# A hybrid encoder layer on one core: first-stage steps at other places, weight remainders on VectorE, output weights in other space

## The chip, the cores and the metric

The kernel is one launch on one core of a Trainium2 chip. The metric is the device time of that core in microseconds (us); lower is better. The engines are PE (TensorE, matmuls; PEld is its weight load), DVE (VectorE), ACT (ScalarE), POOL (GpSimd) and SP (SyncE, which here issues most of the DMA transfers).

## What is computed

Two request groups go through the same layer: a prompt of 2048 rows (16 tiles of 128) and a sample of 8 streams with 16 rows each (one more tile, number 16). All arithmetic is float32. Cut to what matters here:

```python
h   = rmsnorm(x, norm_mix_pre)
P   = h @ w_in                      # q, k, v, z, b, a, B, C, H
q, k, v = silu(causal_dwconv(qkv, width 4)); q, k = l2norm(q), l2norm(k)
beta, g = sigmoid(b), -exp(a_log) * softplus(a + dt_bias)
o, S    = gated_delta_rule(q, k, v, g, beta, S0)   # per chunk: (I + A)^-1, decays, state
o       = rmsnorm_head(o) * silu(z)
y       = B * causal_dwconv(C * H, width 3)
x = x + rmsnorm_post(concat(o, y) @ w_o)
x = x + rmsnorm_post2(swiglu(rmsnorm_pre2(x)))
```

## The kernel before

To keep float32 accuracy, every large matmul is done three times on rounded parts: a tile is split into a rounded copy ("hi", made by ACT) and its remainder ("lo", a subtraction), and hi x hi, hi x lo and lo x hi are summed.

**Three stages.** The first stage (to about 971 us in the profile) makes the input projection and the gated delta rule. The second, `o_tile` (its matmuls are L1008), multiplies by `w_o`. Then come the feed-forward matmuls (L1224, L1382), which the change does not touch.

**The first stage.** The 17 tiles go in five groups: 0 to 2; 3 to 6; 7 to 10; 11, 12 and the sample tile 16; 13 to 15. For each group the 28 column blocks of `w_in` follow each other in the order four k, four q, four z, four v, then four times C, H, B. A block is 24 matmuls (L300), eight k slices with three products each, issued in three parts of 9, 9 and 6. A part with what follows it is a *step*, so that a group has 84 steps, numbered from 0; block n has the steps 3n to 3n+2. Behind a block's last part, `finish_block` takes its result out of PSUM (convolution: R, then acc by three taps at L304, then SiLU into kT, qT or vraw by ACT at L338), and `fetch` asks for the weights three blocks on. The transposes of a k, q or v block (L345) come behind the first part of the block two places later.

**The steps between the blocks.** `plan` writes down at which step each piece of the delta rule is issued. Its function `after(us)` turns a time into a number of steps by an assumed length of a step (2.3 us in group 0, 2.5 or 1.95 in the others). TensorE executes exactly this order (`manual_schedule`); the other engines get an order from the build's scheduler that follows the program's order where the operands allow it. Each engine works through its own queue in order, so that an instruction whose operand is late holds up everything behind it. The pieces are, with their lines:

- `gate_products` (L152 by its helper, scaled at L439 and L440 into xk) and `gate_rates` (three transposes at L447, then small operations); `gate_sums`; `gate_decay`, which sends a row to memory and reads it back as dt;
- `decay_mask` (L516, then an exponential at L518), `decay_scale` (L522), `key_norms`, and per tile `pair_keys`: four products k k^T (L538), taken out into AU by DVE (L539). There are two gbank buffers, so the third pair waits for the first AU;
- `solve_load` (four copies by ACT at L560, a transpose at L562) and `solve`: 31 dependent pairs of small DVE instructions (L571, L573); `solve_store` transposes the result into utd (L578); `level_a` to `level_d` then build the inverse on TensorE (L593, L610, L632, L643);
- `chunk`: per tile four parts that advance the state S; the second to last ends in `out_norm` (L654), the last, `out_turn`, transposes the output (L659) through the single obank, which L684 of the next chunk also uses;
- `sample_start` and `sample_head` in group 3: per head a load of eight states (st, two buffers, L728), two copies by POOL, 16 + 16 matmuls (L736), two further parts, and the stores of the new states;
- `x_rows_load` to `x_split`: rows and columns of the next group.

**Weights.** `weights` fills one of three w2 buffers. In group 0 (for every fourth block in group 1) it reads `w_in` in two halves into one of four wr buffers, ACT rounds each (L277), and L280 subtracts: the first eight second halves on DVE, everything else on POOL. The result is also stored, and later groups only load it (L269).

**The output projection.** Behind the first stage's last block the tiles of `op` and `oa` take the space of the first stage's hi, lo, weight and work tiles; a tile may be written once the tiles under it are done with. Within a pool, tiles lie in the order in which they are first asked for. Weight slices k=0 and k=1 (`early_w`) and the first tile's input (`early_m`) have been loaded before, in `ahead`, into free parts of U, AU, dt, kt, vt and sz. woh0 then lies on hi tiles, which the last block still reads; the staging tiles `wor` lie on work tiles of the convolutions.

`rstd` (L144, L146) is the helper for the inverse root mean square; its two small tiles have a tag from the caller.

Of the kernel before, what the change touches and what calls it, by code (L numbers as in the profile page):

```python
# [9 lines left out]
F32 = mybir.dt.float32  # L10
F32R = mybir.dt.float32r
# [6 lines left out]
P = 128  # L18
D = 1024
# [62 lines left out]
def kernel(  # L82
# [59 lines left out]
    def rstd(small, ss, n, scale, eps, tag):  # L142
        m = small.tile([P, n], F32, tag=tag + "m", name=tag + "m")
        V.tensor_scalar(out=m, in0=ss, scalar1=scale, scalar2=eps, op0=ALU.mult, op1=ALU.add)  # L144
        r = small.tile([P, n], F32, tag=tag + "r", name=tag + "r")
        G.tensor_tensor(out=r, in0=m, in1=neghalf[:, :n], op=ALU.pow)  # L146
        return r
# [9 lines left out]
    with ExitStack() as ph:  # L157
# [101 lines left out]

        wlo = [0]  # L260
        wloads = []
        stores = []

        def weights(j, gi):
            w2 = wp.tile([P, 2, KD, P], F32R, tag="w2", name="w2", bufs=3)
            wh, wl = w2[:, 0], w2[:, 1]
            late = j % 4 == 3
            if not (gi <= late or (gi == RAWG and j % 2)):
                wloads.append(nc.sync.dma_start(out=w2.bitcast(F32), in_=wsplit[j]))  # L269
                while stores:  # L270
                    stores.pop()()
                return wh, wl
            for q in range(2):
                c = slice(4 * q, 4 * q + 4)
                wr = wp.tile([P, KD // 2, P], F32, tag="wr", name="wr", bufs=4)
                wload = nc.sync.dma_start(out=wr, in_=w_in[j, :, c])
                A.copy(wh[:, c], wr)  # L277
                e = V if q and wlo[0] < 8 else G
                wlo[0] += q
                e.tensor_tensor(out=wl[:, c], in0=wr, in1=wh[:, c].bitcast(F32), op=ALU.subtract)  # L280
            wloads.append(wload)
            while stores:
                stores.pop()()
            if gi == late:
                stores.append(lambda: nc.sync.dma_start(out=wsplit[j], in_=w2.bitcast(F32)))
            return wh, wl
# [437 lines left out]
        def sample_head(g, i, h):  # L724
            c = slice(i * P, (i + 1) * P)
            kz, qz, kl, r, yt, o = (smp[nm] for nm in ("kz", "qz", "kl", "r", "yt", "o"))
            st = wk.tile([P, NS, P], F32, tag="st", name="st", bufs=2)
            tc.keep_in_program_order(nc.sync.dma_start(out=st, in_=state[:, h].rearrange("s k v -> k s v")))  # L728
            G.tensor_copy(kz[:, :, 0:LS], sl(g["kT"][h][:, c]))
            G.tensor_copy(qz[:, :, 0:LS], sl(g["qT"][h][:, c]))  # L730
# [38 lines left out]
        def plan(g, nx, events):  # L769
# [3 lines left out]
            def at(t, f, *a):  # L773
                events.setdefault(t, []).append(lambda: f(*a))
# [7 lines left out]
            if gi:  # L782
                at(2, gate_products, g)
            at(5, gate_rates, g)
            t = 5 + after(11)
            at(t, gate_sums, g)
# [4 lines left out]
            at(17, key_norms, g)  # L791
            t += after(6)
            for i in range(n):
# [6 lines left out]
            for b in range(4):  # L800
                at(t + after(5 * b), solve, g, range(8 * b, min(31, 8 * b + 8)))
            t += after(22 if gi else 28)
            at(t, solve_store, g)
            t += after(4)
            for f in (level_a, level_b, level_c, level_d):
# [4 lines left out]
            if npr < n:  # L810
                at(t, sample_start, g, npr)
                for h in range(H):
                    u = t + 1 + 5 * h
                    thread((u, u + 3, u + 5, u + 7, u + 9), sample_head(g, npr, h))
                at(u + 10, lambda: out_norm(g, npr, smp["o"]))
                at(u + 14, lambda: out_turn(g, npr, smp["o"]))
            for i in range(npr):
                thread((t, t + hop, t + 2 * hop, t + 4 * hop), chunk(g, i))
                t += 3 * hop
# [146 lines left out]
        gpost = op.tile([P, D], F32, name="gpost")  # L966
        nc.sync.dma_start(out=gpost, in_=rows_[0].partition_broadcast(P))
        ojunk = op.tile([P, 512], BF16, name="ojunk")
        woh, wol = [], []
        for k in range(KD):  # L970
            wh = oa.tile([P, D], F32R, name=f"woh{k}")
            wl = oa.tile([P, D], F32R, name=f"wol{k}")
            if k < len(early_w):
# [4 lines left out]
            else:  # L978
# [3 lines left out]
                V.tensor_sub(wl, wr, wh.bitcast(F32))  # L982
            woh.append(wh)
            wol.append(wl)

        def o_tile(t):
            if t == 0:
                mr = early_m
            else:
                m = oa.tile([P, KD, P], F32, tag="mr", name="mr")  # L990
                mr = m[:, 0:4], m[:, 4:8]
                nc.sync.dma_start(out=mr[0], in_=mixo[t])
                gi, i = PLACE[t]
                nc.sync.dma_start(out=mr[1], in_=mixs[gi][:, :, i * P:(i + 1) * P])
# [28 lines left out]
            r = rstd(op, ss[:, 2:3], 1, 1.0 / D, EPS, "oy")  # L1023
            hx = op.tile([P, D], F32, tag="hx", name="hx")
            V.tensor_scalar_mul(hx, xt, r)
            ht = op.tile([P, KD, P], F32, tag="ht", name="ht")
            for n in range(2):
# [514 lines left out]
```

## Time and profile before

| what | us |
|---|---|
| median of 3 runs | 2588.16 |
| lowest and highest | 2586.38, 2588.73 |
| the profiled execution's own time | 2589.22 |
| its span, first to last instruction | 2587.4 |
| PE busy | 2487.6 (96%) |
| DVE busy | 1669.2 (65%) |
| ACT busy | 978.7 (38%) |
| POOL busy | 687.0 (27%) |

A line of the profile names the source line, the engine and the tiles written and read: "PE gbank L538 <- DVE AU L539" is a matmul at L538 into gbank that could not start before the DVE instruction at L539 on AU had ended. A table of stretches gives, for each stretch of the span, how long each engine was busy in it, with the number of instructions, and then the mean clock granted to TensorE (1.00 is full), the busy share of the DMA engines and GB/s. Busy times include matmuls at a lowered clock, so that a busy TensorE is not always one at full speed.

### The profile page before, as it was taken

The page shows a single profiled execution, that of the slowest core. Times are in us where ns is not written, and L with a number is a line of the kernel's source. Part 1 is how long each engine was busy: PE and PEld are TensorE (multiplying, and loading weights), DVE is VectorE, ACT ScalarE, POOL GpSimd, SP SyncE. Part 2 cuts the span into 40 slices and gives each one's busy share as a digit, 9 for nine tenths or more (in the row PEclk, how much of TensorE's full clock was granted, in tenths as well). Part 3 has the DMA queues.
Part 4 walks back from the last instruction along what each step waited for, and adds up shares of the span by engine and source line. Part 5 has one row for each costly group of instructions (what it writes and reads, how often), then busy time and mean ns, then how long its engine had stood idle before and what let it go on. Part 6 is the DMA issues. An engine that isn't in the chain of part 4 may idle for free.

```text
span 2587.4 us, 39334 instructions
## 1 busy us (share of the span) xinstructions
PE 2487.6 (96%) x14366; PEld 2271.3 (88%) x14366; DVE 1669.2 (65%) x3044; ACT 978.7 (38%) x2095; POOL 687.0 (27%) x741
## 2 busy tenths in 40 slices
PE   7799999999899999999999999999999999999998
PEld 6788788888888997889999999999999988788786
DVE  6866655755754745777887764544655564777588
ACT  5435424424423414444434442222433245333343
POOL 3353121110110100215556500000000035455563
PEclk9899999999999999999999999999999999999999
DMA  6576365456656556579877788878988853343465
GB/s 231 195 238 248 146 214 193 160 184 216 226 202 206 208 173 208 194 239 319 296 257 269 262 285 257 270 241 254 295 281 284 281 157 116 106 123 124 128 219 185
DMA packets 287393, 561.91 MB, mean 217 GB/s; under 512 B 26652, under 2 KB 175328, under 8 KB 269920
## 3 DMA queue, kind: packets, MB, share of 16 engines
q1 hardware_dynamic: 165808, 483.06, 55.6%
q10 hardware_dynamic: 121392, 76.34, 9.5%
q8 instruction: 113, 1.85, 0.3%
q14 instruction: 80, 0.66, 0.1%
HBM read 400.62 MB, written 158.70 MB: 216 GB/s over the span
## 4 chain that ended last, share of the span: by engine, by line
PE 77%; DVE 12%; DMA 4%; ACT 3%; issue 2%; POOL 1%; ACTq 0%; SPq 0%; DVEq 0%; POOLq 0%
PE fbank L1224 33%; PE dbank L300 20%; PE fbank L1382 11%; PE tbank L1008 3%; PE dbank L1008 3%; DVE Ts L573 1%; DVE pr L571 1%; DVE acc L304 1%; DVE acc L1341 1%; PE gbank L736 1%; PE tbank L345 1%; DMA dr<-in_w_dn 1%; DMA partd<-pt 1%; DVE xr L1401 1%; PE gbank L688 1%
## 5 line engine op out<-in xcount | busy, mean ns | idle before, releaser
L1224 PE MATMUL fbank<-xh,fw 128*128 128x384 f32 (+1 forms) x3696 | 901.2, 327 | 7.7 <-ACT m L1258 3.8
L300 PE MATMUL dbank<-hi,w 128*128 128x384 f32 (+1 forms) x2240 | 681.3, 372 | 9.1 <-ACT w L277 7.6
L1224 PEld LDWEIGHTS fbank<-xh,fw 128*128 128x128 f32 x3696 | 653.6, 189 | 9.1 <-ACT m L1258 4.6
L1224 PE MATMUL fbank<-xl,fw 128*128 128x384 f32 (+1 forms) x1848 | 603.8, 327 | 0.0
L1382 PE MATMUL fbank<-dw,as 128*128 128x512 f32 x1980 | 461.0, 394 | 8.0 <-ACT dw L1079 2.5
L300 PEld LDWEIGHTS dbank<-hi,w 128*128 128x128 f32 x2240 | 423.8, 193 | 47.6 <-ACT w L277 7.6
L1382 PEld LDWEIGHTS fbank<-dw,as 128*128 128x128 f32 x1980 | 371.6, 188 | 97.0 <-ACT dw L1079 3.7
L300 PE MATMUL dbank<-lo,w 128*128 128x384 f32 (+1 forms) x1120 | 407.7, 364 | 1.5 <-DVE lo L213 1.5
L1224 PEld LDWEIGHTS fbank<-xl,fw 128*128 128x128 f32 x1848 | 348.5, 189 | 0.0
L1366 POOL TENSOR_TENSOR as<-ar,as 128x256 fp32r<-128x256 f32 (+1 forms) x207 | 186.5, 911 | 282.4 <-ACT as L1363 281.7
L300 PEld LDWEIGHTS dbank<-lo,w 128*128 128x128 f32 x1120 | 216.0, 193 | 21.2 <-DVE lo L213 4.1
L1341 DVE TENSOR_TENSOR acc<-acc,fbank 128x512 f32<-128x512 f32 x248 | 166.1, 681 | 95.9 <-PE fbank L1382 78.1
L1081 POOL TENSOR_TENSOR dw<-dr,dw 128x512 fp32r<-128x512 f32 x52 | 76.7, 1487 | 484.1 <-ACT dw L1079 483.8
L1363 ACT CAST as<-ar 128x256 fp32r<-128x256 f32 (+1 forms) x288 | 118.2, 427 | 187.2 <-PE fbank L1382 133.6
L304 DVE SCALAR_TENSOR_TENSOR acc<-R,cw,acc 128x384 f32<-128x384 f32 (+2 forms) x180 | 129.0, 719 | 64.9 <-ACT acc L334 58.6
L1199 ACT CAST fw<-rg 128x512 fp32r<-128x512 f32 x124 | 77.3, 623 | 194.1 <-PE fbank L1224 158.3
L1271 DVE TENSOR_TENSOR c<-u,fbank 128x384 f32<-128x384 f32 (+1 forms) x66 | 34.8, 528 | 106.1 <-PE fbank L1224 106.0
L280 POOL TENSOR_TENSOR w<-wr,w 128x512 fp32r<-128x512 f32 x62 | 86.7, 1413 | 60.0 <-ACT w L277 49.9
L1267 DVE TENSOR_TENSOR m<-m,m 128x384 f32<-128x384 f32 (+1 forms) x44 | 23.1, 525 | 93.9 <-ACT m L1260 93.8
L1269 ACT ACTIVATE m<-fbank 128x384 f32<-128x384 f32 (+1 forms) x66 | 31.3, 474 | 129.1 <-PE fbank L1224 126.0
L1200 POOL TENSOR_TENSOR fw<-rg,fw 128x512 fp32r<-128x512 f32 x44 | 70.0, 1591 | 32.7 <-ACT fw L1199 28.7
L1200 DVE TENSOR_TENSOR fw<-rg,fw 128x512 fp32r<-128x512 f32 x80 | 56.4, 706 | 15.6 <-ACT fw L1199 13.2
(360 smaller groups left out, 3488.5 us busy)
## 6 DMA issues: line engine op xcount, KB each, us to landing
w<-wsplit SPq DMA_DIRECT2D x105, 1024.0 KB, 4.9
fw<-fsplit SPq DMA_DIRECT2D x188, 512.0 KB, 4.7
fsplit<-fw SPq DMA_DIRECT2D x94, 512.0 KB, 4.3
partd<-pt ACTq DMA_DIRECT2D x88, 384.0 KB, 6.9
rg<-in_w_gu SPq DMA_DIRECT2D x62, 512.0 KB, 4.1
wsplit<-w SPq DMA_DIRECT2D x28, 1024.0 KB, 4.9
ar<-partd SPq DMA_DIRECT2D x48, 384.0 KB, 3.3
wr<-in_w_in SPq DMA_DIRECT2D x70, 256.0 KB, 4.6
```

The lines of the kernel that those rows point to most:

```text
L280: e.tensor_tensor(out=wl[:, c], in0=wr, in1=wh[:, c].bitcast(F32), op=ALU.subtract)
L300: T.matmul(ps[:, :c], l[:, k, :], r[k][:, :c], start=(k == 0 and r is hi and l is wh), stop=(k == KD - 1 and l is wl))
L304: r = V.scalar_tensor_tensor(acc, raw(d), w[:, d:d + 1], acc, op0=ALU.mult, op1=ALU.add)
L1008: T.matmul(pss[n], m_[:, j, :], w_[k][:, n * 512:(n + 1) * 512], start=(k == 0 and ci == 0), stop=(k == KD - 1 and ci == 2))
L1081: e.tensor_tensor(out=w[:, 1], in0=v, in1=w[:, 0].bitcast(F32), op=ALU.subtract)
L1199: A.copy(w[:, 0], v)
L1200: e.tensor_tensor(out=w[:, 1], in0=v, in1=w[:, 0].bitcast(F32), op=ALU.subtract)
L1224: T.matmul(ps, w_[:, c], b_[k][:, :hw], start=(first and k == 0 and ci == 0), stop=(k == KH - 1 and ci == 2), skip_group_check=not first)
L1341: V.tensor_add(dst, dst, ps)
L1363: ins = A.copy(a[:, 0, :n], v)
L1366: e.tensor_tensor(out=a[:, 1, :n], in0=v, in1=a[:, 0, :n].bitcast(F32), op=ALU.subtract)
L1382: T.matmul(ps, a[:, x_, q * P:(q + 1) * P], w[:, y_], start=(start and q == 0 and ci == 0), stop=(q == c - 1 and ci == 2), skip_group_chec ...
```

## The change

It has four parts.

1. In `weights`, all 70 subtractions go to VectorE; 62 of them were on POOL.
2. In `plan`, steps move. In group 0 `gate_rates` goes from step 5 to 8, and the first pair from 21 to 26, the solve's store from 40 to 45, `level_a` from 42 to 48, the first chunk from 52 to 57. In groups 1 and 2 the first pair goes from 20 to 22, the store from 35 to 39, `level_a` from 37 to 42; the chunks stay at 52. In groups 3 and 4 the store goes from 45 to 47, `level_a` from 48 to 51, the chunks from 57 to 60. A chunk's last part comes two steps later within its chunk. The sample's heads follow each other after seven steps in place of five, and each head's state load is issued two steps ahead of its copies.
3. Ahead of the output projection, the tiles are asked for in another order: hx, ht and mr first, then the weight slices from k=7 down to k=0. So woh0 and wol0 come to lie on the four wr buffers, the other slices from k=1 on the three w2 buffers and then on hi and lo tiles, mh on xk tiles, and the staging `wor` on vraw and xt tiles. The load of gpost moves behind the weight loads.
4. In `rstd`, the first small tile takes only the first letter of the caller's tag, so that two callers in the output projection share one, and the pool is 32 bytes smaller.

```diff
-        m = small.tile([P, n], F32, tag=tag + "m", name=tag + "m")
+        m = small.tile([P, n], F32, tag=tag[0] + "m", name=tag + "m")
...
-                e = V if q and wlo[0] < 8 else G
-                wlo[0] += q
-                e.tensor_tensor(out=wl[:, c], in0=wr, in1=wh[:, c].bitcast(F32), op=ALU.subtract)
+                V.tensor_tensor(out=wl[:, c], in0=wr, in1=wh[:, c].bitcast(F32), op=ALU.subtract)
...
             tc.keep_in_program_order(nc.sync.dma_start(out=st, in_=state[:, h].rearrange("s k v -> k s v")))
+            yield
             G.tensor_copy(kz[:, :, 0:LS], sl(g["kT"][h][:, c]))
...
-            at(5, gate_rates, g)
-            t = 5 + after(11)
+            t = 5 if gi else 8
+            at(t, gate_rates, g)
+            t += after(11)
             at(t, gate_sums, g)
...
             at(17, key_norms, g)
-            t += after(6)
+            t += after(6) + (2 if n == MAXT or not gi else 0)
...
-            t += after(22 if gi else 28)
+            t += after(26 if gi else 28)
             at(t, solve_store, g)
-            t += after(4)
+            t += after(6)
...
-                    u = t + 1 + 5 * h
-                    thread((u, u + 3, u + 5, u + 7, u + 9), sample_head(g, npr, h))
+                    u = t + 1 + 7 * h
+                    thread((u - (2 if h else 0), u, u + 3, u + 5, u + 7, u + 9), sample_head(g, npr, h))
                 at(u + 10, lambda: out_norm(g, npr, smp["o"]))
-                at(u + 14, lambda: out_turn(g, npr, smp["o"]))
+                at(u + 15, lambda: out_turn(g, npr, smp["o"]))
             for i in range(npr):
-                thread((t, t + hop, t + 2 * hop, t + 4 * hop), chunk(g, i))
+                thread((t, t + hop, t + 2 * hop, t + 4 * hop + 2), chunk(g, i))
...
-        nc.sync.dma_start(out=gpost, in_=rows_[0].partition_broadcast(P))
         ojunk = op.tile([P, 512], BF16, name="ojunk")
-        woh, wol = [], []
+        spare = [op.tile([P, D], F32, tag="hx", name="hx"), op.tile([P, KD, P], F32, tag="ht", name="ht"),
+                 oa.tile([P, KD, P], F32, tag="mr", name="mr")]
+        wo = {k: [oa.tile([P, D], F32R, name=f"{nm}{k}") for nm in ("woh", "wol")] for k in reversed(range(KD))}
+        woh, wol = ([wo[k][q] for k in range(KD)] for q in range(2))
         for k in range(KD):
-            wh = oa.tile([P, D], F32R, name=f"woh{k}")
-            wl = oa.tile([P, D], F32R, name=f"wol{k}")
+            wh, wl = wo[k]
...
+        nc.sync.dma_start(out=gpost, in_=rows_[0].partition_broadcast(P))
```

The first `o_tile` that uses hx, ht and mr takes the three tiles of `spare`.

More of the change, by code (lines that the diff above doesn't have):

```diff
@@ L258, in x_split @@
             split(nx["xk"][k], k, len(tiles) * P, nx["hi"], nx["lo"])
-        wlo = [0]
         wloads = []
@@ L982 @@
                 V.tensor_sub(wl, wr, wh.bitcast(F32))
-            woh.append(wh)
-            wol.append(wl)
+        nc.sync.dma_start(out=gpost, in_=rows_[0].partition_broadcast(P))
         def o_tile(t):
@@ L989, in o_tile @@
             else:
-                m = oa.tile([P, KD, P], F32, tag="mr", name="mr")
+                m = oa.tile([P, KD, P], F32, tag="mr", name="mr") if t > 1 else spare[2]
                 mr = m[:, 0:4], m[:, 4:8]
@@ L1023, in o_tile @@
             r = rstd(op, ss[:, 2:3], 1, 1.0 / D, EPS, "oy")
-            hx = op.tile([P, D], F32, tag="hx", name="hx")
+            hx = op.tile([P, D], F32, tag="hx", name="hx") if t else spare[0]
             V.tensor_scalar_mul(hx, xt, r)
-            ht = op.tile([P, KD, P], F32, tag="ht", name="ht")
+            ht = op.tile([P, KD, P], F32, tag="ht", name="ht") if t else spare[1]
             for n in range(2):
```

## The prediction

> **What bounds the kernel now.** I read the page first, then the waits of TensorE between 21 and 981 us (the first stage without its start), then a table of stretches, then single lines.
>
> ```profile
> span 2587.4 us, 39334 instructions
> ```
>
> ```profile
> PE gbank L538 <- DVE AU L539: 11.5, 3, 6.3
> PE gbank L593 <- DVE utd L578: 11.0, 3, 5.2
> PE gbank L736 <- DMA st<-in_state: 8.3, 2, 4.8
> PE tbank L345 <- DVE R L311: 5.3, 1, 5.3
> PE tbank L345 <- ACT qT L338: 4.9, 4, 3.2
> PE gbank L447 <- ACT xk L440: 3.8, 1, 3.8
> PE dbank L1008 <- ACT mh L1002: 3.7, 1, 3.7
> PE tbank L345 <- ACT kT L338: 2.8, 3, 2.2
> PE obank L659 <- DVE o L684: 2.5, 2, 2.1
> PE obank L659 <- DVE o L654: 2.3, 1, 2.3
> ```
>
> These ten rows say that TensorE sat idle some 56 us, in about a dozen places, and who ended each wait (columns: total us, times, longest). The change moves the steps behind most of them. Next the stretches: first the groups 0, 1, 3 and 4, then a window around each wait. Columns: length, busy PE, PEld, DVE, ACT, POOL, then the granted clock.
>
> ```profile
> 0.00:217.00 217.00, 180.63 (x1156) 167.92 (x1157) 154.24 (x297) 97.53 (x190) 90.41 (x101) 0.93 0.67 233
> 217.00:424.00 207.00, 201.97 (x1246) 168.57 (x1245) 127.81 (x259) 82.80 (x156) 41.44 (x57) 0.98 0.54 192
> ```
> ```profile
> 624.00:818.00 194.00, 176.60 (x1164) 167.81 (x1162) 114.33 (x302) 64.56 (x158) 22.09 (x52) 0.95 0.60 205
> 818.00:971.00 153.00, 149.18 (x1086) 144.48 (x1084) 85.74 (x213) 55.27 (x116) 16.56 (x37) 0.99 0.57 199
> 33.00:42.00 9.00, 6.18 (x23) 6.05 (x24) 5.60 (x18) 7.04 (x11) 0.61 (x2) 0.62 0.41 161
> 60.00:126.00 66.00, 49.81 (x316) 47.64 (x315) 57.55 (x118) 28.17 (x48) 29.90 (x31) 0.88 0.55 188
> 71.00:90.00 19.00, 9.41 (x35) 8.58 (x35) 14.00 (x22) 9.78 (x13) 5.39 (x7) 0.73 0.40 149
> 116.00:131.00 15.00, 8.64 (x164) 7.57 (x162) 11.04 (x23) 8.07 (x16) 6.51 (x11) 0.66 0.53 176
> 165.00:172.00 7.00, 4.85 (x20) 3.55 (x19) 3.75 (x5) 0.99 (x3) 3.06 (x2) 0.76 0.82 267
> 263.00:271.00 8.00, 5.42 (x25) 4.38 (x24) 4.46 (x8) 1.93 (x4) 0.27 (x2) 0.79 0.00 0
> 300.00:308.00 8.00, 5.56 (x80) 4.60 (x80) 4.05 (x12) 4.76 (x8) 0.51 (x1) 0.79 0.01 2
> 470.00:477.00 7.00, 4.42 (x28) 3.63 (x27) 4.76 (x8) 2.19 (x4) 0.37 (x2) 1.00 0.08 12
> 703.00:715.00 12.00, 6.77 (x102) 6.19 (x102) 5.96 (x17) 6.37 (x16) 0.49 (x2) 0.72 0.41 145
> 770.00:780.00 10.00, 6.51 (x35) 6.38 (x35) 4.30 (x10) 0.63 (x1) 0.83 (x3) 0.66 0.78 270
> 790.00:800.00 10.00, 5.25 (x27) 5.29 (x28) 0.04 (x1) 0.00 (x0) 0.00 (x0) 0.66 0.34 118
> 896.00:906.00 10.00, 6.70 (x164) 5.92 (x162) 4.44 (x11) 5.00 (x10) 0.64 (x2) 0.83 0.27 103
> 971.00:981.00 10.00, 6.32 (x16) 4.97 (x17) 6.25 (x9) 5.83 (x9) 0.00 (x0) 0.66 0.71 229
> ```
>
> A wait costs more than its idle time: in eleven of these twelve windows the granted clock fell too. I price a window as length minus PE busy, plus PE busy times (1 minus clock). 71:90 gives 9.6 + 9.41 x 0.27 = 12.1 us. In order of time: 33:42 5.2; 71:90 12.1; 116:131 9.3; 165:172 3.3; 263:271 3.7; 300:308 3.6; 470:477 2.6; 703:715 7.1; 770:780 5.7; 790:800 6.5; 896:906 4.4; 971:981 5.8. Together **69.3 us**; with the 2.3 us for L654, 71.6 us. No more than that is to be had here.
>
> By the Trainium skill, TensorE: Matmul & The Clock Gate, section "HAM oscillation", only idle gaps over about 3.4 us throttle the clock. Idle of 2.15, 2.58 and 2.44 us (165:172, 263:271, 300:308) came with clocks of 0.76 to 0.79 here, and 2.58 us at 470:477 with 1.00, so the measurement decides and short gaps can count. By the rule those three windows and 896:906 (3.30 us idle) would lose 4.6 us less, and the forecast below would be about 2549.
>
> **The change, part by part.** A step is a third of a block; a group has 84. From PE busy over 84, one lasts about 2.15 us in group 0, 2.4 in 1 (and 2), 2.1 in 3, 1.8 in 4.
>
> *Remainders to VectorE.* 62 subtractions leave POOL:
>
> ```profile
> L280 POOL TENSOR_TENSOR w<-wr,w x62: 1257/1298/1748, 7.6 to 402.1; 128x512 fp32r<-128x512 f32 x62
> ```
> ```profile
> L280 DVE TENSOR_TENSOR w<-wr,w x8: 676/1362/1732, 8.1 to 55.9; 128x512 fp32r<-128x512 f32 x8
> ```
>
> Undisturbed, VectorE takes 0.68 us: 62 x 0.68 = 42.2 us more for it, 48 of the 62 in group 0. Against that stands what POOL does to VectorE. The same 31 + 31 solve instructions (L571, then L573), in group 0 with 12 POOL remainders beside them and in group 4 with none:
>
> ```profile
> 87.00:123.50 36.50, 12.38 (x31) 0.92 0.53 173
> 871.00:900.00 29.00, 7.86 (x31) 1.00 0.60 218
> ```
> ```profile
> 87.00:123.50 36.50, 12.96 (x31) 0.92 0.53 173
> 871.00:900.00 29.00, 8.62 (x31) 1.00 0.60 218
> ```
> ```profile
> 87.00:123.50 36.50, 14.33 (x12) 0.92 0.53 173
> ```
>
> 25.3 against 16.5 us: 8.9 us lost to 12 remainders, 0.74 each; the 12 would cost VectorE 8.2. So I take the move as **zero** for VectorE's load, with ends of +42.2 us (no relief) and -3.7 us (62 x 0.06). A block's weights are fetched two blocks ahead, about 10 us in group 0; that covers a remainder queued behind the solve unless VectorE lags further than that.
>
> By the Trainium skill, TensorE: Matmul & The Clock Gate, section "Architectural detail", VectorE's queue is strictly first in, first out, so a remainder cannot pass the taps and solve steps ahead of it. No row here shows such a lag reaching a block's weights; if it did by some 5 us once, the forecast would be about 2550.
>
> *Group 0's gate step, 5 to 8 (window worth 5.2).* The transposes at L447 no longer wait for the gates' scaling.
>
> ```profile
> 35.82 0.50 PE L447 MATMUL gbank<-cst,xk 16*128 16x16 f32 x3 [3.76 <-ACT xk L440]
> ```
> ```profile
> 37.08 0.52 ACT L338 ACTIVATE kT<-acc 128x384 f32<-128x384 f32 x1
> ```
>
> TensorE is free at 35.82 - 3.76 = 32.06 and now runs block 2's first nine matmuls, until about 34. What is late next is the transposition of the first k block, which needs kT, done at 37.6. So the wait mostly changes its name. Gain **2** (0 to 5.2).
>
> *Group 0's pairs, solve and levels, five or six steps later (windows 71:90 and 116:131, worth 21.4).* For the third pair, five steps are 10 us against 6.3 of idle, and the decay mask behind it comes only three steps later. But 60:126 shows VectorE busy 57.55 of 66 us, so this stretch can shrink by little more than the 8.5 us in which VectorE idles. And the solve's store, from step 40 to 45, now stands behind the taps of two more v blocks. TensorE will still wait before the levels, only with more blocks behind it. Gain **8** (-5 to 18).
>
> *A chunk's last part two steps later.* The output transposes no longer stand in front of L684 and L654: two steps are 4 us against 2.1 and 2.3 us of idle. Gain **3** in group 0 (of 3.3) and **1.5** in group 3 (of 2.3), ends zero and the whole.
>
> *Groups 1 and 2.* Pairs two steps later (4.8 us, idle 2.6 each); levels five steps later (12 us, idle 2.4); the chunks stay at step 52, so there is slack behind. Group 1's 14 remainders net to zero as above. Gains **7** of 7.3 (4 to 7.3) and **2.5** of 2.6 (1 to 2.6).
>
> *Groups 3 and 4: levels three steps later.* 6.3 and 5.4 us against 5.23 and 3.30 us of idle, so the move alone covers them. But the solve's store goes from step 45 to 47, behind the last v block's three taps of about 0.6 us each: the wait returns by up to 2 us, with its clock. Gains **4** of 7.1 (1 to 7.1) and **3** of 4.4 (1 to 4.4).
>
> *Sample heads every seven steps instead of five, each state load two steps ahead of its copies (windows 770:780 and 790:800, worth 12.2).*
>
> ```profile
> DMA to landing us min/median/max: 6.7/6.8/7.1
> ```
>
> With two buffers, head h+2's load waits for head h's store. Between that store and the matmuls on the loaded state lie eight steps (70 to 78) in place of four (67 to 71): 8 x 2.1 = 17 us, of which the load takes 7. The load waits in SP's queue with block weights behind it; the ring of three w2 covers that. POOL's two copies go with the later part. Gain **11** (6 to 12.2).
>
> *The output projection (window worth 5.8).* Now the first cast waits for the last block's end:
>
> ```profile
> 971.93 0.62 ACT L976 CAST woh<-U 128x512 fp32r<-128x512 f32 x1 [3.84 <-DVE yo L423]
> ```
>
> After the change, k=0's halves lie on the weight staging that groups 0 and 1 alone use, and mh on x tiles done with before the last blocks; only k=1 lies on the last block's weights. Cast k=0 ahead, and TensorE starts at once; k=1's two casts (1.2 us) hide behind k=0's six matmuls. The loads for k=2 and 3 go onto finished v and x tiles; k=6 and 7 may be a little late. gpost, now last on SP, is wanted only after the first tile's matmuls. Gain **4.5** (1 to 5.8).
>
> *What is given back.* Head 3 of the sample and its output now fall on steps 1 to 13 of group 4, among gates and k blocks, and group 0's last 30 steps hold what 36 held. The early load of the sample's share of sz on SP waits for that output, ten steps later than before, with block weights behind it. I charge **3** (0 to 8). The shared tag in rstd shifts addresses and costs nothing: its two users follow each other in one chain.
>
> **Sum:** 2 + 8 + 3 + 1.5 + 7 + 2.5 + 4 + 3 + 11 + 4.5 = 46.5, less 3 = 43.5 us. The profiled execution took 2589.2 us (span 2587.4), 1.1 above the median of 2588.2; 2589.2 - 43.5 - 1.1 = 2544.6, so **2545 us**, 2530 to 2560 within this case.
>
> **Rivals.**
>
> *All waits go* (chance 0.15): 71.6 us, 2517. For it: every shift is longer than its idle. Against it: VectorE's 57.55 of 66 us, and kT at 37.6.
>
> *The waits change their names* (0.25): groups 0, 3, 4 and the projection end where they end now, because the same producer is late for the next step too. Left are 7 + 2.5 + 11 = 20.5 us: 2568. For it: the gate step, and the solve's store behind more taps. Against it: in groups 3 and 4 the shift is about three times the extra taps.
>
> *Slower* (0.05): VectorE becomes the bound of groups 0 and 1 because the long durations are not POOL's doing. Then 42.2 us are added whole and those two groups gain nothing; against them stand 2.5 + 4 + 1.5 + 3 + 11 + 4.5 = 26.5 us elsewhere. 15.7 us net: 2604. It decides below a relief of 0.25 us for each remainder (42.2 - 62 x 0.25 = 26.7); the rows above give 0.74.
>
> *No difference* (0.03): some queue behind the moved steps takes back what they give, 2588.
>
> **Chances and range.** Forecast 0.52; with the first two rivals, faster by over 0.2% has 0.92. About 0.2% is what a measurement of this kernel can tell from no change. Within it 0.03, slower 0.05. The range of **2518 to 2574** leaves out the last two cases, some of the first rival's low side and some of the second's high side, 0.19 in all.
>
> **What would show it.** L280 on VectorE should take 0.68 to 0.75 us throughout and the solve in group 0 about 17 us. The waits on AU, in_state and o at L659 should vanish; kT should take over from xk near 34 us; utd should remain in group 0 and shrink to at most 2 us in groups 3 and 4; woh's first cast should start before the last block's end. The forecast is wrong if TensorE in group 0 waits for L280, if group 4's first 13 steps show new waits of several us, or if the clock stays low where idle time is gone.

## The result, and the profile after

The changed kernel takes 2563.0 us (median of 5 runs, 2558.7 to 2570.2) against 2586.4 for the kernel before in the same session: a ratio of 0.9913, with a 95% interval of 0.989 to 0.9936. That is 22.5 us saved (17 to 28), where 43.5 were forecast. The profiled execution took 2558.9 us.

From the page of the changed kernel: the span is 30.3 us shorter, POOL is busy 80 us less, and VectorE's sum stands where it was, although 62 more subtractions run on it.

```profile
span 2557.1 us, 39320 instructions
...
PE 2469.6 (97%) x14366; PEld 2254.5 (88%) x14366; DVE 1667.9 (65%) x3106; ACT 976.7 (38%) x2095; POOL 607.3 (24%) x679
```

TensorE's waits in the first stage of the changed kernel (total us, times, longest). Up to about line 700 the numbers are three lower than before (L590 was L593, L342 was L345), further down one lower (L1007 was L1008).

```profile
PE gbank L590 <- DVE utd L575: 14.2, 2, 13.9
PE obank L699 <- DVE ot L658: 7.8, 7, 2.1
PE tbank L342 <- ACT qT L335: 7.4, 4, 4.5
PE tbank L342 <- ACT kT L335: 4.8, 3, 2.7
PE dbank L1007 <- ACT mh L1001: 3.7, 1, 3.7
PE gbank L607 <- ACT xs L593: 2.3, 1, 2.3
```

The waits on AU, in_state and o at L659 (now L656) have gone. Three stand out in their place: one of 13.9 us for utd, where three made 11.0 before; a new one, for ot, in seven places; and mh, to the tenth what it was.

Now the stretches of the first stage, cut at each group's first gate product, so that each row is one group (length, then busy PE, PEld, DVE, ACT, POOL, clock). Before:

```profile
28.80:217.10 188.30, 162.95 (x1084) 153.93 (x1083) 139.16 (x269) 85.38 (x167) 81.00 (x85) 0.92 0.64 221
217.10:424.00 206.90, 201.87 (x1245) 168.56 (x1244) 127.81 (x259) 82.80 (x156) 41.44 (x57) 0.98 0.54 192
424.00:623.70 199.70, 197.12 (x1245) 165.90 (x1244) 116.17 (x260) 73.89 (x140) 21.61 (x45) 1.00 0.52 180
623.70:818.10 194.40, 177.00 (x1165) 168.03 (x1164) 114.33 (x302) 64.64 (x158) 22.09 (x52) 0.95 0.60 205
818.10:974.70 156.60, 149.10 (x1087) 144.44 (x1084) 88.39 (x217) 58.03 (x122) 16.56 (x37) 0.99 0.57 199
```

And after:

```profile
31.20:216.80 185.60, 156.52 (x1084) 148.33 (x1083) 138.10 (x313) 84.24 (x167) 23.85 (x41) 0.93 0.63 224
216.80:419.00 202.20, 199.38 (x1245) 166.50 (x1244) 126.55 (x273) 82.69 (x156) 22.25 (x43) 1.00 0.55 197
419.00:619.70 200.70, 197.75 (x1245) 166.09 (x1244) 115.17 (x260) 74.12 (x140) 22.04 (x45) 1.00 0.52 179
619.70:793.40 173.70, 169.03 (x1157) 161.36 (x1156) 110.63 (x294) 63.87 (x155) 22.11 (x51) 0.99 0.66 227
793.40:947.00 153.60, 149.68 (x1094) 144.71 (x1091) 92.19 (x226) 58.34 (x125) 17.54 (x38) 1.00 0.61 212
```

Group 3 gave 20.7 us, group 1 4.7, group 4 3.0, group 0 only 2.7, and group 2 lost 1.0. So two thirds of the gain lie in the group that holds the sample's heads, and group 0, for which 13 us had been forecast, gave next to nothing. These lengths repeat better than whole times: group 4 takes 153.6, 153.6 and 153.7 us in the changed kernel and in runs 1 and 3 below, which leave it alone, and group 2 takes 200.7, 200.7 and 200.5. So the experiments are read by them first. They come from one execution of each kernel, though. The two shown here are 30.3 us apart, where all runs together give 22.5, so that the lengths add up to more than the saving.

### The profile page after: what moved, and what is told of

It is laid out like the page before. It is cut to its first block, busy times and chain, and to the rows that moved or that the text cites. A ratio compares the mean times of both kernels' runs of the same rounds, so it can differ in the third digit from the quotient of the medians.

```text
span 2557.1 us, 39320 instructions
## 1 busy us (share of the span) xinstructions
PE 2469.6 (97%) x14366; PEld 2254.5 (88%) x14366; DVE 1667.9 (65%) x3106; ACT 976.7 (38%) x2095; POOL 607.3 (24%) x679
## 4 chain that ended last, share of the span: by engine, by line
PE 78%; DVE 11%; DMA 4%; issue 3%; ACT 2%; POOL 1%; ACTq 0%; SPq 0%; DVEq 0%; POOLq 0%
PE fbank L1223 32%; PE dbank L297 21%; PE fbank L1381 12%; PE tbank L1007 3%; PE dbank L1007 3%; DVE acc L1340 1%; DMA xt<-in_x 1%; PE tbank L342 1%; DVE acc L301 1%; DVE xr L1400 1%; PE obank L699 1%; DMA partd<-pt 1%; PE gbank L734 1%; POOL dw L1080 1%; PE obank L679 1%
## 5 line engine op out<-in xcount | busy, mean ns | idle before, releaser
L301 DVE SCALAR_TENSOR_TENSOR acc<-R,cw,acc 128x384 f32<-128x384 f32 (+2 forms) x180 | 121.2, 675 | 58.8 <-ACT acc L331 51.8
L323 POOL COPY hist<-R 128x3 f32<-128x3 f32 x60 | 21.3, 355 | 190.3 <-ACT R L306 164.0
```

The source lines that it names most:

```text
L301: r = V.scalar_tensor_tensor(acc, raw(d), w[:, d:d + 1], acc, op0=ALU.mult, op1=ALU.add)
```

## The experiments

Ratios are to the kernel before, timed beside each run; the brackets are 95% intervals.

**1 and 2: the remainders.** First the changed kernel with the old division, then the old kernel with the new one.

```diff
+                e = V if q and wlo[0] < 8 else G
+                wlo[0] += q
-                V.tensor_tensor(out=wl[:, c], in0=wr, ...
+                e.tensor_tensor(out=wl[:, c], in0=wr, ...
```

> The changed kernel with the old division of the weight remainders (the first eight second halves on VectorE, the other 54 on POOL). My theory: what VectorE spends on the remainders it saves on its other two-input operations, so the move nets to zero; the time stays within 5 us of the changed kernel (2558 to 2568), VectorE's busy sum within 10 us of 1668, the remainders' mean on POOL again near 1.3 us. Rival: the remainders standing in VectorE's queue between the solve's steps are what keeps group 0's wait for utd at 13.95 us; then this kernel is 8 to 18 us faster and that wait is under 5 us.

> The kernel before with one edit: all remainders on VectorE. My theory (net zero): within 5 us of the kernel before, VectorE's busy sum within 10 us of 1669, its remainders at 0.68 us in place of a median of 1.36. Rival (VectorE pays the 42 us, no relief): 15 to 40 us slower. Second rival (relief larger than price, VectorE being on the path of group 0): 5 to 12 us faster, with the lengths of groups 0 and 1 shorter.

Measured: 2578.0 us (ratio 0.9964, 0.9952 to 0.9977) for the old division in the changed kernel, so the move is worth 0.0051, some 13 us, there. Alone in the kernel before it gives 2580.0 us (0.9969, 0.9959 to 0.998), 8 us. My theory of a net zero falls in both, and so does the rival of a burden: taking the remainders back made the wait for utd shorter (7.1 us), yet groups 0 and 1 longer. In the second run the second rival's time and lengths came true (group 0 181.2 us against 188.3, group 1 203.5 against 206.9), but of its reasons only that VectorE is on group 0's path: the relief is not larger than the price, as the sums will show.

Groups 0 and 1 with the old division in the changed kernel (185.6 and 202.2 us without it):

```profile
28.90:224.10 195.20, 160.56 (x1084) 152.05 (x1083) 139.08 (x269) 83.96 (x167) 77.65 (x85) 0.92 0.62 213
224.10:434.40 210.30, 202.71 (x1244) 168.62 (x1243) 127.34 (x259) 82.57 (x156) 40.79 (x57) 0.98 0.54 189
```

VectorE is busy as long as in the changed kernel (139.1 against 138.1 us in group 0, 1667.7 against 1667.9 in all; 1669.2 before against 1669.8 in run 2), so the sum is indeed zero. But work of the same sum is done later. Where, shows group 0 up to the solve's first step, which comes at 87.7 us before and at 78.5 with the new division alone. VectorE's groups there (instructions, then busy us, mean ns), in the kernel before:

```profile
L304 DVE SCALAR_TENSOR_TENSOR acc<-R,cw,acc 128x384 f32<-128x384 f32 x24 | 16.7, 711 | 1.4 <-POOL rt L528 1.0 <-ACT acc L336 0.2
L280 DVE TENSOR_TENSOR w<-wr,w 128x512 fp32r<-128x512 f32 x4 | 5.8, 1459 | 5.1 <-ACT w L277 5.1
L516 DVE SCALAR_TENSOR_TENSOR dt<-dt,nG,cst 128x128 f32<-128x128 f32 x12 | 5.3, 509 | 0.0
L311 DVE TENSOR_TENSOR R<-dbank,rb 128x384 f32<-128x384 f32 x8 | 4.3, 548 | 1.5 <-PE dbank L300 1.5
```

and with all remainders on VectorE:

```profile
L301 DVE SCALAR_TENSOR_TENSOR acc<-R,cw,acc 128x384 f32<-128x384 f32 x24 | 14.3, 610 | 1.2 <-ACT acc L333 1.1
L277 DVE TENSOR_TENSOR w<-wr,w 128x512 fp32r<-128x512 f32 x14 | 9.0, 687 | 2.6 <-ACT w L276 2.6
L308 DVE TENSOR_TENSOR R<-dbank,rb 128x384 f32<-128x384 f32 x8 | 4.3, 552 | 0.8 <-PE dbank L297 0.8
L513 DVE SCALAR_TENSOR_TENSOR dt<-dt,nG,cst 128x128 f32<-128x128 f32 x12 | 3.2, 349 | 0.0
```

Ten more remainders cost 3.2 us (5.8 to 9.0), since the four that were there fall from 1.46 to 0.69 us. The taps get 2.4 back and the decay mask 2.1, both on the chain to the solve. The stretch is 9.2 us shorter (58.9 to 49.7); VectorE works 3.5 us less in it and idles 5.7 less (14.5 to 8.8). That the chain, and not the sum, is what counts is read from these rows; no run takes the contention off the chain alone. L311 took 548 and takes 552 ns: it reads PSUM and one SBUF tile, the others two SBUF tiles. By the Trainium skill, GPSIMD Engine Reference, section "Specifications", POOL contends with VectorE instructions that have two SBUF inputs; the rows agree, input by input.

**3: group 0's steps back.**

```diff
-            t = 5 if gi else 8
+            t = 5
-            t += after(6) + (2 if n == MAXT or not gi else 0)
+            t += after(6) + (2 if n == MAXT else 0)
-            t += after(6)
+            t += after(6) if gi else after(4)
             for f in (level_a, ...
```

> The changed kernel with group 0's steps as before: gate rates at step 5 instead of 8, pairs, solve and levels five or six steps earlier. My theory: in group 0 the later steps gave nothing, since utd only came later too; within 4 us of the changed kernel (2559 to 2567), group 0's length 184 to 190 against 185.6, the wait for utd 12 to 17 us. Rival (the forecast's own terms for group 0, 2 + 8 + 3): 8 to 13 us slower.

Measured: 2551.9 us (0.9858, 0.984 to 0.9876), 11 to 14 us **faster** than the changed kernel. Both theories fall: these steps do not gain and are not neutral, they cost. Group 0 and its wait, with the steps as before:

```profile
32.30:207.70 175.40, 158.98 (x1084) 151.50 (x1083) 139.21 (x313) 85.06 (x167) 23.90 (x41) 0.94 0.67 237
```
```profile
PE gbank L590 <- issue: 5.2, 1, 5.2
```

The profile names nobody for this wait ("issue"), but utd's transposition ends at 119.3 us and TensorE goes on at 119.4, so it is the wait for utd. 10.2 us of length, of which this wait is 13.9 - 5.2 = 8.7. Groups 1 and 3 give back 2.7 and 1.7 us (204.9 and 175.4 us). Where the 8.7 come from, the solve's second instruction tells (31 of them; first and last start), in the changed kernel and with the old steps:

```profile
L570 DVE TENSOR_TENSOR Ts<-Ts,pr x31: 176/258/296, 96.6 to 134.2; 128x126 f32<-128x126 f32 x3, 128x30 f32<-128x30 f32 x2, 128x56 f32<-128x56 f32 x2, 128x78 f32<-128x78 f32 x2
```
```profile
L570 DVE TENSOR_TENSOR Ts<-Ts,pr x31: 174/259/933, 83.0 to 118.0; 128x126 f32<-128x126 f32 x3, 128x30 f32<-128x30 f32 x2, 128x56 f32<-128x56 f32 x2, 128x78 f32<-128x78 f32 x2
```

Five steps put the solve's start back by 13.6 us and its end by 16.2. TensorE came to the levels at 121.5 (135.5 less 13.95) in place of 114.2 (119.4 less 5.2): six steps brought it only 7.3 us later. (Group 0 starts at 31.2 us in the one trace and at 32.3 in the other; counted from there, each shift is 1.1 us larger.) The third pair (73.9 us with the old steps) used to stand ahead of TensorE's wait for qT, which ends at 82.6; five steps later (86.5) it stands behind that wait, which now ends at 81.2. So the solve now starts after it and its half clock (granted 0.50 from 81.3 to 86.0 us). This run undoes the gate step, the pairs, the levels and the chunks of group 0 together; no run moves the gate step alone.

**7: only the levels later.** If the steps before the solve are the harm, the levels' shift alone should do good.

```diff
-            t += after(6) if gi else after(4)
+            t += after(6) if gi else after(4) + 3
             for f in (level_a, ...
```

> The changed kernel with group 0's gate rates, pairs and solve at the old, early steps and only the solve's levels three steps later. Theory now (a step of group 0 is 1.7 us of TensorE without waits, not the 2.1 that the forecast took; moving the solve's start back costs more than the levels' shift covers): three steps of 1.7 us cover the 5.2 us that TensorE waits for utd with early steps, and its half clock, so 4 to 8 us faster than the kernel with all of group 0's steps undone (2551.85), that is 2544 to 2548; wait for utd under 1 us. Rival (the solve's end slides with the work that is put in front of it, as it did with the whole move): utd comes as much later, the wait stays 4 to 6 us and the time within 3 us of 2552.

Measured: 2552.9 us (0.9865, 0.9848 to 0.9882), the same as with all steps back; group 0 takes 176.5 us against 175.4. The rival holds. The wait, and the solve:

```profile
PE gbank L590 <- issue: 4.3, 1, 4.3
```
```profile
L570 DVE TENSOR_TENSOR Ts<-Ts,pr x31: 169/258/941, 79.2 to 117.7; 128x126 f32<-128x126 f32 x3, 128x30 f32<-128x30 f32 x2, 128x56 f32<-128x56 f32 x2, 128x78 f32<-128x78 f32 x2
```

The solve's span grew from 35.0 to 38.5 us, since one more v block's work (evacuation, three taps, two remainders and the scaling) now stands between its steps. Three steps later for TensorE shortened the wait by 0.9 us.

**4: a chunk's last part one step later instead of two.**

```diff
-                thread((t, t + hop, t + 2 * hop, t + 4 * hop + 2), chunk(g, i))
+                thread((t, t + hop, t + 2 * hop, t + 4 * hop + 1), chunk(g, i))
```

> The changed kernel with a chunk's last part one step later than before the change, not two. My theory: with two steps it falls into the step in which the next chunk's third part writes the single bank that VectorE's ot is still reading, which is TensorE's seven waits on ot of 7.8 us; one step puts it between, so 5 to 8 us faster (2555 to 2558) and TensorE's wait on ot at most 1 us. Rival (the waits change their names): the output transposes then stand in front of o again, some 2 us each in groups 0 and 3, and the time stays within 2 us.

Measured: 2554.7 us (0.987, 0.9857 to 0.9884), so the theory holds; the wait on ot fell from 7.8 to 0.7 us, groups 1 and 2 from 202.2 and 200.7 to these:

```profile
219.90:418.40 198.50, 198.50 (x1245) 166.25 (x1244) 125.54 (x273) 82.70 (x156) 23.23 (x43) 1.00 0.56 201
418.40:616.30 197.90, 197.22 (x1245) 165.86 (x1244) 115.22 (x260) 74.05 (x140) 22.31 (x45) 1.00 0.52 182
```

Why two steps collide, the timeline of the changed kernel shows in group 1 (start, duration, instruction, in brackets the idle time before it and its end):

```profile
375.82 0.27 PE L656 MATMUL obank<-cst,o 128*128 128x128 f32 x1
...
377.57 0.75 DVE L658 SCALAR_TENSOR_TENSOR ot<-obank,vec,sz 128x512 f32<-128x512 f32 x1
...
378.37 1.16 PE L699 MATMUL obank<-yt,dt 128*128 128x128 f32 x8 [1.38 <-DVE ot L658]
```

With chunks six steps apart and hop at two, a last part at t + 10 falls on the step of the next chunk's third part, t + 6 + 4. L699 wants the one obank while VectorE still reads the transposed output from it. One step sets them apart. It is not free: groups 0 and 3 grew by 1.8 and 0.8 us (187.4 and 174.5), so that by lengths the edit is worth 4.3 us in all, and 8 to 11 by whole times.

**5: the sample's heads alone**, in the kernel before (the three hunks of the diff on `sample_head`).

> The kernel before with the sample heads' part alone (heads every seven steps, each state load two steps ahead of its copies, the turn one step later). My theory: it is the largest single gain, 10 to 13 us; the two waits on in_state (8.3 us) and the half clock behind them go; the stretch of group 3 shrinks from 194.5 to 181 to 185 us, group 4's does not grow by more than 2. Rival (the forecast's given-back term, heads now colliding with group 4's gates): group 4 grows by 5 us or more and the whole gain stays under 7.

Measured: 2576.5 us (0.9963, 0.995 to 0.9976), 9.6 us; the waits on in_state are gone. Groups 3 and 4, against 194.4 and 156.6 before:

```profile
622.50:804.10 181.60, 171.50 (x1161) 163.86 (x1159) 112.05 (x296) 64.49 (x156) 21.08 (x51) 0.97 0.63 216
804.10:963.50 159.40, 151.79 (x1091) 146.35 (x1089) 90.52 (x223) 58.38 (x124) 17.72 (x38) 0.98 0.58 199
```

The gain is 12.8 us, and 2.8 are given back in group 4. Group 4 grew more than the "2" that I allowed and less than the rival's 5; the whole gain, 9.6, is just under the theory's 10 and above the rival's 7. So the theory stands in its mechanism and is a little high in both numbers.

**6: the space as before.** The hunks on `rstd`, `spare`, `wo` and gpost were undone.

> The changed kernel with the output weights' space, gpost's place and the tag in rstd as before. My theory: the early space gave nothing, because the first cast still starts after the last block's end, behind stores in ScalarE's queue, and mh behind the casts; within 3 us of the changed kernel, group 4's stretch 153 to 157 and the wait for mh about 3.7 us. Rival (the forecast's 4.5 us): 4 to 6 us slower, nearly all of it at the projection's start and in the o stage.

Measured: 2563.3 us (0.9914, 0.9898 to 0.993), no difference, as the theory said; group 4 takes 153.7 against 153.6 us, the wait for mh 3.7 against 3.7. The space bought nothing by itself.

**8: POOL's old load beside VectorE's new one.**

```diff
+                wlo[0] += q
+                if not q or wlo[0] > 8:
+                    dm = wp.tile([P, 512], BF16, tag="dm", name="dm", bufs=1)
+                    G.tensor_tensor(out=..., in0=wh[:, c].bitcast(F32), in1=wh[:, c].bitcast(F32), op=ALU.subtract)
```

> The changed kernel with an extra subtraction on POOL for each weight half whose remainder POOL computed before (54 in all, same inputs and size, the result unused): VectorE keeps all remainders, POOL's load and its sharing with VectorE come back. This measures the relief alone. If POOL's two-input operations are what made VectorE's operations long: VectorE's busy sum grows by 30 to 50 us and groups 0 and 1 by 10 to 30 us together. If instead the gain of moving the remainders came from the weights being ready earlier: the busy sum stays within 10 us of 1668 and the time within 5 us of the changed kernel.

Measured: 2589.4 us (1.0013, 1.0004 to 1.0022), 26 us slower than the changed kernel. The page's busy line, its rows for the extra subtractions and for the remainders, and group 0 (185.6 without):

```profile
PE 2477.2 (96%) x14366; PEld 2260.1 (87%) x14366; DVE 1704.1 (66%) x3106; ACT 976.8 (38%) x2095; POOL 692.4 (27%) x741
...
L282 POOL TENSOR_TENSOR dm<-w 128x512 bf16<-128x512 f32 x62 | 86.5, 1395 | 80.7 <-ACT w L277 79.0
...
L278 DVE TENSOR_TENSOR w<-wr,w 128x512 fp32r<-128x512 f32 x70 | 65.2, 954 | 5.9 <-ACT w L277 5.3
```
```profile
30.10:237.90 207.80, 163.49 (x1085) 153.88 (x1084) 167.83 (x313) 84.63 (x167) 83.13 (x85) 0.89 0.58 200
```

There are 62 extra subtractions, as many as POOL lost; the 54 in the expectations of runs 1 and 8 is a miscount. VectorE is busy 36.2 us longer: 0.58 us for each. That is the price of POOL's neighbourhood, apart from who computes what, and it is near the 0.68 us that VectorE pays for a remainder. But 17.1 of the 36.2 us are the remainders' own (65.2 against 48.1 us in the changed kernel), which stood on POOL before. So this run shows the contention and its size; the zero sum itself is shown by the busy sums of runs 1 and 2. In group 0, nine taps that overlap a subtraction on POOL take 1.26 us on average and the 35 others 0.61; of the evacuations, which read PSUM and one SBUF tile, three that overlap one take 0.54 us, as the nine others do. 22.2 of the 26 us are in group 0, and none of its matmuls' waits there is for a weight, so late weights are not the reason.

**9, 10 and 11: together.** Group 0's steps back and one step for the last part (9). Then (10), POOL issues the last stores in place of ScalarE and the first mh comes ahead of the k=1 casts; and (11), as 9, with the solve emitted at one step.

```diff
-                nc.scalar.dma_start(out=mixs[g["gi"]][:, h, :], in_=yo[:, :c])
+                (nc.gpsimd if g["gi"] == 4 and h == 3 else nc.scalar).dma_start(...
...
         for k in range(KD):
             wh, wl = wo[k]
+            if k == 1:
+                first.append(mix(early_m[0]))
```
```diff
-                at(t + after(5 * b), solve, g, range(8 * b, min(31, 8 * b + 8)))
+                at(t + (after(5 * b) if gi else 0), solve, g, range(8 * b, min(31, 8 * b + 8)))
```

> Two of the findings together: the changed kernel with all of group 0's steps as before the change and a chunk's last part one step later instead of two. Theory: the two are independent (group 0's length; TensorE's waits on ot in groups 0, 1 and 2), so their gains add: 2563.0 less 11.2 (the run with group 0's steps undone) less 8.3 (the run with one step) = 2543.5, 2540 to 2548. Rival: with group 0's chunks back at their earlier steps the last part needs the second step there; the waits on o come back in group 0 (2 to 4 us with their clock) and the time is 2547 to 2552.

> The combined kernel with one more edit at the output projection: the last tile's two stores and the short convolution's state are issued by POOL in place of ScalarE, and the first tile's first mh stands ahead of the k=1 casts that wait for the last block. Theory: what kept TensorE waiting 3.75 us was ScalarE's queue, not the space; the first cast then starts before the last block's end, the wait for mh goes and with it a 3.41 us stretch of half clock: 3 to 5.5 us faster than the combined kernel. Rival (k=0's halves or mh are themselves late, or TensorE then waits as long for wol or k=1): the wait takes another name and the time is within 2 us of the combined kernel.

> The combined kernel with group 0's 31 solve steps emitted at one step (the first of the four) instead of four. Theory: the wait for utd is set by how much other work of VectorE is queued between the solve's instructions, not by the step at which the solve or the levels stand; less stands between them now, so the solve's span falls from 35.5 to 25 to 30 us and the wait for utd from 5.2 to under 2 us. Whether that pays is open: by that theory 0 to 6 us faster than the combined kernel if the taps behind it have slack, and 3 to 10 us slower if TensorE then waits for vraw instead.

Measured: 2539.7 us (0.9815, 0.9799 to 0.9832), just under the range of the sum; then 2534.4 us (0.9803, 0.9785 to 0.982), and 2544.5 us (0.9825, 0.9807 to 0.9843). The early start brings 3 to 5 us by whole times, whose intervals overlap; the length shows it, for group 4 goes from 153.2 to 149.3 us. ScalarE at the end of the first stage of the changed kernel:

```profile
943.03 0.33 ACTq L659 DMA_DIRECT2D mixo<-ot  x1
943.89 0.33 ACTq L425 DMA_DIRECT2D mixs<-yo  x1
944.27 0.62 ACT L976 CAST woh<-U 128x512 fp32r<-128x512 f32 x1 [4.37 <-DVE yo L420]
...
946.35 0.61 ACT L1001 CAST mh<-vt 128x512 fp32r<-128x512 f32 x1
...
947.02 0.79 PE L1007 MATMUL dbank<-woh,mh 128*128 128x512 f32 x1 [3.75 <-ACT mh L1001]
```

The first cast idles 4.37 us "until yo", which it does not read: two stores ahead of it in ScalarE's queue wait for ot and yo. With those stores on POOL:

```profile
917.77 0.60 ACT L986 CAST woh<-U 128x512 fp32r<-128x512 f32 x1
...
918.80 0.61 ACT L974 CAST mh<-vt 128x512 fp32r<-128x512 f32 x1
...
921.08 0.39 PE L1013 MATMUL dbank<-woh,mh 128*128 128x512 f32 x1
```

TensorE goes on without this wait; what it has left is 0.8 us for wol a little later. The early cast needs the space of the change, since woh0 lay before on hi tiles that the last block still reads. So the space should pay only together with the queue; no run has the queue's edit without the space.

Experiment 11 tested nothing. Between the solve's start and utd, VectorE's instructions came in the very order of 9, since the build's scheduler places them; the solve's span (35.1 us) and the wait for utd (5.2) are those of 9. What its 2544.5 against 2539.7 us does show is how far medians of one order of work lie apart.

**12: two of group 0's four pk copies on POOL**, in kernel 10.

```diff
-                A.copy(pk[r, :, :4 * n], ...
+                (G.tensor_copy if g["gi"] == 0 and b > 1 else A.copy)(pk[r, :, :4 * n], ...
```

> The combined kernel with the early start of the output projection, and two of group 0's four pk copies (0.85 us each, ahead of two qT in ScalarE's queue) moved to POOL. Theory: group 0's wait for qT (6.0 us in the trace of the last kernels) is ScalarE's queue: four pk copies of 0.85 and a table load of 1.28 stand ahead of the first qT. With two copies the wait falls by 1.5 to 2 us, the solve starts 0 to 1.7 us earlier and group 0 is 1.5 to 4 us shorter (170 to 172.5 against 174.0); the whole time 2530 to 2535. Rival (POOL's copies end later than ScalarE's did, or they slow VectorE beside them): the solve starts later by 1 us or more, the wait for utd grows by as much, and group 0 stays at 173 us or above.

Measured: 2538.9 us (0.9803, 0.9788 to 0.9819), no difference; group 0 takes 174.2 against 174.0 us. Its first two waits:

```profile
PE gbank L590 <- issue: 6.5, 1, 6.5
PE tbank L342 <- ACT qT L335: 5.7, 3, 4.3
```

The wait for qT is 4.3 us where run 10 has 6.0, as forecast. But that is not shown to be the edit's doing: in runs 3 and 11, which lack it, this wait is 4.5 and 4.4 us. The solve starts no earlier, 50.5 us behind the group's first gate product against 49.8 in run 10, and the wait for utd is 6.5 us against 5.2. So the rival's outcome came, in smaller numbers: the solve is 0.7 us later, not earlier, and group 0 stays above 173 us.

## Why the prediction held in its range and failed in its parts

| step of the forecast | forecast us | measured us | by |
|---|---|---|---|
| group 0: gates 2, pairs to levels 8 | +10 | -10.2 | length, run 3 to the changed kernel |
| group 0: last part later | +3 | +5.8 | length, run 2 to run 3 (181.2 to 175.4) |
| remainders | 0 | +10.5 (whole times: +8 alone, +13 in the change) | length of groups 0 and 1, before to run 2; runs 2 and 1 |
| group 1 | +7 | +1.3; +5.0 with one step | length, run 2 (203.5) to after; to run 4 |
| group 2 | +2.5 | -1.0; +1.8 with one step | length, before to after; to run 4 |
| group 3: levels 4, last part 1.5 | +5.5 | +7.9 | length, run 5 to after |
| group 4: levels | +3 | +5.8 | length, run 5 to after |
| heads | +11 | +12.8 | length, before to run 5 |
| output projection | +4.5 | 0 | run 6 |
| given back | -3 | -2.8 | group 4, before to run 5 |

With two steps, as in the change, the measured lengths add up to 30.1 us.

**The total** lies in the wide range, 18 us above the predicted time. It is 3 us outside the 2530 to 2560 that the forecast gave for its own case, and nearer to the 2568 of the second rival, the waits that change their names. That rival is right for the projection and too mild for group 0; it is wrong for groups 3 and 4, which gained, and for group 1, of whose 7 us only 1.3 came. So no account on record fits as a whole, and that the total lies in the range is in good part luck: a loss of 20 us against the forecast in group 0 and a gain of 8 to 13 that the forecast had put at zero partly offset each other.

**The step that failed** is "group 0's pairs, solve and levels, five or six steps later", gain 8. It took TensorE's steps as 2 us of relief each. But the prediction had the reason against it in its own row: VectorE busy 57.55 of 66 us. With each block that TensorE does ahead of the levels, that block's VectorE work goes between the solve's steps (run 7), so later levels buy almost nothing, and later pairs only start the solve later (run 3). Its lower bound, -5, was too mild: the pairs also passed TensorE's wait for qT.

**Remainders at zero.** The sum was right (1667.7 us against 1667.9), the conclusion was not: the gain of 8 to 13 us lies even outside the ends set for the term, 3.7 us at best. In a stretch where a dependent chain on VectorE sets the time, it matters which instructions are stretched: POOL lengthened the taps, the mask and the solve, while a remainder on VectorE is done mostly some 10 us ahead of its block's first matmul in group 0 of the changed kernel (from the second block on 2.4 us at the least) and can fill gaps. In the solve itself the sum does come out at nothing: 34.5 us long before, 35.3 in run 2.

**A chunk's last part.** The gain in group 0 was there (in group 3 no run parts it from the levels'); that two steps meet the next chunk's third part in every group was overlooked. It cost 3.7 and 2.8 us in groups 1 and 2, and so explains most of the shortfall there.

**The projection.** The space did come free and k=0's cast depends on nothing late. The step failed at "cast k=0 ahead": the cast's queue had two stores with late operands in front, and mh stood behind k=1's casts.

**Heads, levels of groups 3 and 4, given back** were right in mechanism. The heads and what is given back were nearly right in size; the levels brought more than forecast, in group 4 5.8 us where 4.4 was the upper end.

Of the marks set in advance, L280's successor takes 0.68 us in the median (0.71 on average, 1.53 at the longest), the waits on AU, in_state and o are gone, and utd costs groups 3 and 4 next to nothing (14.2 us in all, 13.9 of them in group 0). kT took over from xk: 4.4 us in two waits before 60 us. The two tiles made 6.0 before, but also 3.8 in run 3, where the gate step is back, so the step gained nothing. The clock is 0.99 to 1.00 in groups 1, 3 and 4, and group 4's first steps show no new wait. The solve of group 0 is 15.6 us of instructions, but spread over 38. For the remainders TensorE's weight load waits 0.2 us, once. The mark that failed is woh's first cast: it starts at 944.3 us, behind the last block. What stays open is why whole times of run 3 gain 11 to 14 us where its groups give 5.9 in all and its trace is 5.1 us shorter; the stretch of the feed-forward, which no run touches, varies by more than that difference (below).

## What to carry to other kernels

Two operations of equal cost are not worth the same: take the contention off the chain that others wait for, and put the work that is wanted late into its gaps. A consumer moved behind other blocks gains little if those blocks feed the same busy engine that makes its operand, as in group 0; keep the start of that chain early, and count what each extra block puts between its links. And before a step is moved by n, look which step of its neighbour already uses the same buffer n later, and what stores stand ahead of it in its queue.

## What was not expected of the hardware

POOL lengthens VectorE's taps also with plain copies of 32 partitions. In run 12, four taps took 3.47 us beside two such copies, two of them 0.61 us, as undisturbed, and two 1.19 and 1.18:

```profile
76.55 3.47 DVE L301 SCALAR_TENSOR_TENSOR acc<-R,cw,acc 128x384 f32<-128x384 f32 x4
...
76.76 2.19 POOL L557 COPY pk<-AU 32x384 f32<-32x384 f32 x2 [2.80 <-DVE AU L536]
```

The feed-forward stretch, the same code in all runs, took 924.7 us in the changed kernel and 932.6 in run 1, a difference that is not of the change:

```profile
1151.60:2076.30 924.70, 916.77 (x5562) 914.78 (x5561) 584.89 (x923) 324.04 (x669) 195.37 (x135) 1.00 0.83 272
```
```profile
1167.60:2100.20 932.60, 919.10 (x5562) 916.23 (x5561) 583.64 (x923) 323.44 (x669) 199.51 (x135) 1.00 0.82 270
```
